# A top-256 search moved onto VectorE as a count over integers, with accumulator-freeing work given precedence

## The chip, the core and the metric

The kernel runs on one core of one Trainium2 chip. Five engines each work through their own queue of instructions in order: TensorE (PE in the rows; its weight loads are PEld), VectorE (DVE), ScalarE (ACT), GpSimd (POOL) and SyncE (SP), which mostly issues transfers. The metric is device microseconds of one execution, the median of several runs.

## What is computed

One layer of a hybrid encoder block over 1024 frames of width 1024, in float32. The part that matters here is the sparse attention: for each frame an index score over all earlier frames is worked out, the 256 best are kept, and attention looks at those alone.

```python
mod = silu(c) @ w_ada + b_ada                      # shift, scale, gate for both halves of the layer
h = rms_norm(x, g_mix) * (1 + sc1) + sh1
proj = h @ w_in                                    # attention columns, then RWKV columns
...
rel = relu(einsum('bthd,bsd->bths', q_idx, k_idx)) # 8 index heads
score_idx = einsum('bth,bths->bts', w_idx, rel)
score_idx = where(key_pos < limit, score_idx, -inf)
_, sel = top_k(score_idx, 256)                     # the search of this change
...                                                # softmax attention over the selected frames; RWKV-7 time mixing
x = x + gt1 * (concat(o_a, o_b) @ w_out)
u = relu(h2 @ w_ff1);  x = x + gt2 * ((u * u) @ w_ff2)
```

## The kernel before

The frames are worked on in two halves of 512 (hf 0 and 1). The program text goes: projection and RWKV of half 0; attention projections of half 0; index scores and search of half 0 (`indexer(0)`); RWKV projections of half 1 (`rwkv_proj(1)`); attention of half 0; RWKV of half 1; attention projections of half 1; then the output projection of half 0 and its feed-forward `ffn(0)`, with `indexer(1)`, attention of half 1, output projection and norm of half 1 hooked in at certain of its 64 units; and last `ffn(1)`.

The order of each engine's queue is fixed before the kernel runs. A planner walks the program with its own estimate of how long each instruction takes, and on each engine puts next whichever instruction is ready by that estimate and has the highest precedence. Precedence is the place in the program text: what stands earlier goes first, and later work fills the gaps. So the matrix products of `ffn(0)` fill TensorE while `indexer(1)` and attention of half 1, which stand earlier, run on other engines. At run time nothing is reordered: an instruction whose input is late holds up all behind it on its engine.

All big products go through `dense` (L389 to L399): for 128 output columns it takes eight weight tiles, split by ACT (L382) and POOL or DVE (L384) into a high and a low part, and runs 24 matmuls of 512 columns into one PSUM accumulator `ps_mm`, of which there are two. A product with its 24 matmuls is called a unit here. What empties the accumulator differs: in `shifted` (L419) ACT reads it (L422) and DVE reads it again (L426, L427); in `out_proj` DVE adds it to the residual (L1029); in the first eight units of each group of sixteen of `ffn`, ACT reads it with a relu (L1060), squares (L1074), rounds (L1075), and DVE subtracts (L1076); in the other eight DVE adds it to the residual (L1082).

The search (L846 to L913) finds for each frame, a row on one of 128 partitions, the 256th largest score. It does so bit by bit from 31 to 0: a candidate threshold is made, the scores at or above it are counted, and the bit is kept if at least 256 are. Half 0 has two blocks of rows (384 and 512 scores a row), half 1 four blocks (640, 768, 896 and 1024). In half 0 the first block and in half 1 the first two are counted by DVE; the others by ACT, with a sign and a running sum (L873). For the upper 16 bits DVE counts on a bf16 copy of the scores' upper halves (L858, L879, a one-source instruction), for the lower 16 on the scores themselves (L881, a two-source instruction with a tile of zeros). Small instructions of one or two columns (L870, L871, L888, L894 to L896) make the next candidates; DVE runs them for ACT's blocks too. After the search the masks are built (L914 to L928).

Of the kernel before, what the change touches and what calls it, by code (L numbers as in the profile page):

```python
# [15 lines left out]
HALF = 512  # L16
# [93 lines left out]
def body(tc, I, out, dbg=None):  # L110
# [305 lines left out]
        while held:  # L416
            nc.scalar.dma_start(*held.pop(0))

    def shifted(hf, hT, mi, col0, dst=None):  # L419
        ps = proj(hf, hT, OFF_B + col0, 128)  # L420
        t1 = dp.tile([128, HALF], F32, name="sh1", tag="sh1", bufs=2)
        A.activation(t1, ps, AF.Identity, scale=omu[:, mi:mi + 1])  # L422
        release()
        y = dst if dst is not None else dp.tile([128, HALF], F32, name="shy", tag="shy", bufs=2)
        mu = P("mu", mi, mi + 1)
        V.scalar_tensor_tensor(y[:, 1:HALF], ps[:, 0:HALF - 1], mu, t1[:, 1:HALF], ALU.mult, ALU.add)  # L426
        V.scalar_tensor_tensor(y[:, 0:1], lastp[:, hf, mi:mi + 1], mu, t1[:, 0:1], ALU.mult, ALU.add)  # L427
        if hf == 0:
            A.copy(lastp[:, 1, mi:mi + 1], ps[:, HALF - 1:HALF])
        return y  # L430
# [357 lines left out]
    def indexer(hf, ap, mp):  # L788
# [30 lines left out]
        for h in range(8):  # L819
# [5 lines left out]
            for b in blocks:  # L825
                W = width(b)
                s_ = sc[b]
                for c0 in range(0, W, 512):
                    n = min(512, W - c0)
                    ps = pst("f")  # L830
                    tq = slice(b * 128, b * 128 + 128)
                    mmul(ps[:, 0:n], qs[:, tq], kiH[:, c0:c0 + n], start=True, stop=False)
                    mmul(ps[:, 0:n], qs[:, tq], kiL[:, c0:c0 + n], start=False, stop=True)
                    rl = ap.tile([128, 512], F32, name="rl", tag="rl", bufs=3)
                    A.activation(rl[:, 0:n], ps[:, 0:n], AF.Relu)
                    if h == 0:
                        V.tensor_scalar(s_[:, c0:c0 + n], rl[:, 0:n], wn[hf][:, b, 0:1], None, ALU.mult)
                    else:
                        V.scalar_tensor_tensor(s_[:, c0:c0 + n], rl[:, 0:n], wn[hf][:, b, h:h + 1],
                                               s_[:, c0:c0 + n], ALU.mult, ALU.add)  # L840
# [2 lines left out]

        vb = [b for i, b in enumerate(blocks) if (i in VB if hf else i == VB0)]  # L846
        ab = [b for b in blocks if b not in vb]
        nv, na = len(vb), len(ab)
        jk = ap.tile([128, SW], BF16, name="jk", tag="jk", bufs=1)
        jka = ap.tile([128, SW], BF16, name="jka", tag="jka", bufs=1)  # L850

        def small(nm, n, dt=F32):
            return ap.tile([128, n], dt, name=nm, tag=nm, bufs=1)

        top = {}
        for b in vb:
            tp = ap.tile([128, width(b)], BF16, name=f"top{b}", tag=f"top{b}", bufs=1)
            V.tensor_copy(tp, sc[b].bitcast(BF16).rearrange("p (n two) -> p n two", two=2)[:, :, 1])  # L858
            top[b] = tp
        cv, cand, acc, pre, xm, xmh = (small("cv", nv), small("cand", nv, I32), small("acc", nv, I32),  # L860
                                       small("pre", nv, I32), small("xm", nv, I32), small("xmh", nv, I32))
        ca, canda, acca, prea, xma = (small("ca", na), small("canda", na, I32), small("acca", na, I32),
                                      small("prea", na, I32), small("xma", na, I32))
        zer = ap.tile([128, SW], BF16, name="zer", tag="zer", bufs=1)
        V.memset(zer, 0.0)
        V.memset(pre, 0)
        V.memset(prea, 0)
        for bit in range(31, -1, -1):
            if bit < 31:
                V.scalar_tensor_tensor(cand, pre, 1 << bit, xmh if bit >= 16 else xm, ALU.bitwise_or, ALU.bitwise_xor)  # L870
                V.scalar_tensor_tensor(canda, prea, 1 << bit, xma, ALU.bitwise_or, ALU.bitwise_xor)  # L871
            for i, b in enumerate(ab):
                A.activation(jka[:, 0:width(b)], sc[b], AF.Sign, scale=-1.0,  # L873
                             bias=0.0 if bit == 31 else canda.bitcast(F32)[:, i:i + 1], accum_out=ca[:, i:i + 1])
            for i, b in enumerate(vb):
                src = top[b] if bit >= 16 else sc[b]
                thr = 0.0 if bit == 31 else cand.bitcast(F32)[:, i:i + 1]
                if bit >= 16:
                    V.tensor_scalar(jk[:, 0:width(b)], src, thr, 0.0, ALU.is_ge, ALU.add, accum_out=cv[:, i:i + 1])  # L879
                else:  # L880
                    V.scalar_tensor_tensor(jk[:, 0:width(b)], src, thr, zer[:, 0:width(b)], ALU.is_ge, ALU.add,  # L881
                                           accum_out=cv[:, i:i + 1])

            for i, b in enumerate(ab):
                if bit == 31:
                    V.tensor_scalar(xma[:, i:i + 1], ca[:, i:i + 1], width(b) - 510.5, -1.0, ALU.is_gt, ALU.mult)
                else:
                    V.tensor_scalar(acca[:, i:i + 1], ca[:, i:i + 1], width(b) - 510.5, float(1 << bit),  # L888
                                    ALU.is_le, ALU.mult)
            if bit == 31:  # L890
                V.tensor_scalar(xm, cv, TOPK - 0.5, -1.0, ALU.is_lt, ALU.mult)
                V.tensor_scalar(xmh, xm, -65536, None, ALU.bitwise_and)
            else:
                V.tensor_scalar(acc, cv, TOPK - 0.5, float(1 << bit), ALU.is_ge, ALU.mult)  # L894
                V.tensor_tensor(pre, pre, acc, ALU.bitwise_or)  # L895
                V.tensor_tensor(prea, prea, acca, ALU.bitwise_or)  # L896
        V.tensor_tensor(cand, pre, xm, ALU.bitwise_xor)
        V.tensor_tensor(canda, prea, xma, ALU.bitwise_xor)
        for i, b in enumerate(ab):
            V.tensor_scalar(jk[:, 0:width(b)], sc[b], canda.bitcast(F32)[:, i:i + 1], 0.0, ALU.is_gt, ALU.add,  # L900
                            accum_out=ca[:, i:i + 1])

        up, lo16, cy = small("up", na), small("lo16", na, I32), small("cy", na)
        V.tensor_scalar(up, ca, TOPK - 0.5, None, ALU.is_ge)
        V.tensor_scalar(lo16, prea, 65535, None, ALU.bitwise_and)
        V.tensor_tensor(lo16, lo16, up, ALU.add)
        V.tensor_scalar(cy, lo16, 65535.5, None, ALU.is_ge)
        V.tensor_scalar(lo16, lo16, 65535, None, ALU.bitwise_and)
        V.tensor_scalar(prea, prea, 16, None, ALU.logical_shift_right)
        V.tensor_tensor(prea, prea, cy, ALU.add)  # L910
        V.tensor_scalar(prea, prea, 16, None, ALU.logical_shift_left)
        V.tensor_tensor(prea, prea, lo16, ALU.bitwise_or)
        V.tensor_tensor(canda, prea, xma, ALU.bitwise_xor)  # L913
        need = small("need", nb)  # L914
        for i, b in enumerate(blocks):
            W = width(b)
            th = (cand if b in vb else canda).bitcast(F32)
            ii = (vb if b in vb else ab).index(b)
            th = th[:, ii:ii + 1]
            gt = jk[:, 0:W]  # L920
            V.tensor_scalar(gt, sc[b], th, 0.0, ALU.is_gt, ALU.add, accum_out=need[:, i:i + 1])
            V.tensor_scalar(need[:, i:i + 1], need[:, i:i + 1], -1.0, float(TOPK), ALU.mult, ALU.add)
# [101 lines left out]
    def out_proj(hf, xT, mh, ml):  # L1024
        mark('oproj%d' % hf)
        GRP[0] = 4 + hf
        for d in range(8):
            ps = dense(I["w_out"], 0, 8, d * 128, 128, lambda k: mh[:, k, :], lambda k: ml[:, k, :])
            V.scalar_tensor_tensor(xT[:, d, :], ps, mod[:, 16 + d:17 + d], xT[:, d, :], ALU.mult, ALU.add)  # L1029

    def ffn(hf, xT, hT, fp, xp, hid, hooks={}):
        mark('ffn%d' % hf)
# [19 lines left out]
        for fg in range(FF // 128 // GF):  # L1052
            uh, ul = [], []
            for f in range(GF):
                hook(16 * fg + f)
                ps = dense(I["w_ff1"], 0, 8, (fg * GF + f) * 128, 128,
                           lambda k: hT[0][:, k, :], lambda k: hT[1][:, k, :])
                r = fp.tile([128, HALF], F32, name="ur", tag="s2", bufs=SB)
                if RL[hf] == "a":
                    A.activation(r, ps, AF.Relu)  # L1060
                else:
                    V.tensor_scalar(r, ps, 0.0, None, ALU.max)
                if f < 4:
                    ta, tb = (("shy", "fsq"), ("shy", "fsq"), ("sh1", "arn"), ("sh1", "cT"))[f]
                    a = dp.tile([128, HALF], F32R, name="uh", tag=ta, bufs=2)
                    b = dp.tile([128, HALF], F32R, name="ul", tag=tb, bufs=2 if f < 2 else 1)
                else:
                    a = hid.tile([128, HALF], F32R, name="uh", tag="uh", bufs=4)
                    b = hid.tile([128, HALF], F32R, name="ul", tag="ul", bufs=4)
                if SQ[hf] == "v":  # L1070
                    A.activation(a, r, AF.Square)
                    V.tensor_tensor(r, r, r, ALU.mult)
                else:
                    A.activation(r, r, AF.Square)  # L1074
                    A.copy(a, r)  # L1075
                V.tensor_tensor(b, r, a.bitcast(F32), ALU.subtract)  # L1076
                uh.append(a)
                ul.append(b)
            for d in range(8):
                hook(16 * fg + 8 + d)  # L1080
                ps = dense(I["w_ff2"], fg * GF * 128, GF, d * 128, 128, lambda k: uh[k], lambda k: ul[k])
                V.scalar_tensor_tensor(xT[:, d, :], ps, mod[:, 40 + d:41 + d], xT[:, d, :], ALU.mult, ALU.add)  # L1082
                if hf and fg == FF // 128 // GF - 1 and d in (5, 7):
                    store(d // 6)
        if not hf:
# [198 lines left out]
```

## Time and profile before

| What | Value |
|---|---|
| median of 3 runs | 1809.81 us (1807.12 to 1810.46) |
| the profiled execution, its own time | 1806.42 us |
| span of the profiled execution | 1804.6 us |
| TensorE busy, share of the span | 89% |
| VectorE | 64% |
| ScalarE | 48% |
| GpSimd | 27% |
| mean granted TensorE clock | 0.966 |

The span is the time from the first to the last instruction; the execution's own time is a little longer. Busy shares are averages over stages with different limits. Matmuls are pipelined, and one is shown as busy until its modelled end, so that a busy TensorE can still be slower than at its best: how many matmuls it ends in a stretch says more than its busy time.

### The profile page before, as it was taken

To read this page: it belongs to the slowest core of one execution; us is meant where nothing else is said; L and a number is where in the kernel's file an instruction comes from. 1 tells how busy PE (TensorE), PEld (TensorE's weight loads), DVE (VectorE), ACT (ScalarE), POOL (GpSimd) and SP (SyncE) were. 2 spreads that over 40 slices of the span, in tenths; PEclk is the share of its full clock that TensorE was granted. 3 is DMA by queue.
4 is the path that set the end of the run, shared out by engine and by line. 5 is a ranking of instruction groups with operands and counts; after the bars stand their busy time and mean duration, and the time that the engine had idled before them with its cause. 6 is when DMAs were issued, how large, how long until landed. Compare 5 with 4: busy or idle time off the path is not lost. (4 is left out here: it accounts for less than half of the span.)

```text
span 1804.6 us, 25007 instructions
## 1 busy us (share of the span) xinstructions
PE 1613.8 (89%) x8388; PEld 1206.4 (67%) x8388; DVE 1159.7 (64%) x2981; ACT 859.5 (48%) x1760; POOL 480.3 (27%) x391
## 2 busy tenths in 40 slices
PE   5996888898778988898987888999999999999998
PEld 3684655666554656665665676777886788888887
DVE  4788789956998779876899739773213333333333
ACT  3323353445556655344854783775335252525251
POOL 2445323334331143323223344111444300000000
PEclk9998899999989999999988998999999999999999
DMA  8896254225436533111212234223432343333332
GB/s 309 257 297 188 83 159 123 86 71 144 114 91 173 182 120 104 53 48 43 74 47 64 65 94 117 83 82 98 143 100 70 96 133 94 100 94 100 94 96 74
DMA packets 279493, 205.83 MB, mean 114 GB/s; under 512 B 33811, under 2 KB 234515, under 8 KB 279366
## 3 DMA queue, kind: packets, MB, share of 16 engines
q1 hardware_dynamic: 268610, 185.00, 34.5%
q10 hardware_dynamic: 10628, 19.24, 2.9%
q8 instruction: 66, 1.08, 0.3%
q14 instruction: 61, 0.50, 0.1%
q0 software_dynamic: 128, 0.01, 0.0%
HBM read 175.42 MB, written 28.78 MB: 113 GB/s over the span
## 5 line engine op out<-in xcount | busy, mean ns | idle before, releaser
L384 POOL TENSOR_TENSOR wlo<-wraw,whi 128x512 fp32r<-128x512 f32 x256 | 350.9, 1375 | 699.4 <-ACT whi L382 583.7
L119 PE MATMUL ps_mm<-hh,whi 128*128 128x512 f32 (+1 forms) x1024 | 421.9, 413 | 25.6 <-ACT whi L382 6.0
L119 PE MATMUL ps_mm<-hl,whi 128*128 128x512 f32 (+1 forms) x1024 | 420.4, 411 | 3.8 <-DVE hl L372 1.4
L119 PE MATMUL ps_mm<-hh,wlo 128*128 128x512 f32 (+1 forms) x1024 | 420.6, 411 | 3.5 <-POOL wlo L384 3.4
L382 ACT CAST whi<-wraw 128x512 fp32r<-128x512 f32 x384 | 235.1, 616 | 393.7 <-PE ps_mm L119 369.9
L119 PEld LDWEIGHTS ps_mm<-hh,whi 128*128 128x128 f32 (+1 forms) x1024 | 197.1, 193 | 74.5 <-ACT whi L382 13.5
L119 PEld LDWEIGHTS ps_mm<-hh,wlo 128*128 128x128 f32 (+1 forms) x1024 | 197.5, 193 | 47.6 <-POOL wlo L384 6.6
L119 PEld LDWEIGHTS ps_mm<-hl,whi 128*128 128x128 f32 (+1 forms) x1024 | 197.6, 193 | 47.3 <-issue 6.2
L119 PE MATMUL ps_mm<-uh,whi 128*128 128x512 f32 x512 | 205.0, 401 | 16.0 <-DVE pre L895 5.1
L119 PE MATMUL ps_mm<-ul,whi 128*128 128x512 f32 x512 | 204.8, 400 | 5.7 <-DVE ul L1076 5.7
L119 PE MATMUL ps_mm<-uh,wlo 128*128 128x512 f32 x512 | 203.8, 398 | 0.6 <-POOL wlo L384 0.6
L384 DVE TENSOR_TENSOR wlo<-wraw,whi 128x512 fp32r<-128x512 f32 x128 | 88.3, 690 | 130.1 <-ACT whi L382 130.1
L873 ACT ACTIVATE jka<-sc,canda 128x1024 bf16<-128x1024 f32 (+1 forms) x93 | 90.2, 970 | 89.8 <-DVE canda L871 77.4
L119 PEld LDWEIGHTS ps_mm<-uh,whi 128*128 128x128 f32 x512 | 97.8, 191 | 41.3 <-issue 9.7
L1082 DVE SCALAR_TENSOR_TENSOR xT<-ps_mm,mod,xT 128x512 f32<-128x512 f32 x64 | 47.9, 749 | 117.9 <-PE ps_mm L119 117.9
L119 PEld LDWEIGHTS ps_mm<-ul,whi 128*128 128x128 f32 x512 | 98.0, 191 | 29.2 <-DVE ul L1076 7.3
L119 PEld LDWEIGHTS ps_mm<-uh,wlo 128*128 128x128 f32 x512 | 97.8, 191 | 23.3 <-POOL wlo L384 1.1
L1076 DVE TENSOR_TENSOR ul<-ur,uh 128x512 fp32r<-128x512 f32 x64 | 44.0, 690 | 74.6 <-ACT uh L1075 74.4
L616 DVE TENSOR_TENSOR ytmp<-Lu,Y 128x60 f32<-128x60 f32 (+24 forms) x248 | 75.2, 303 | 6.1
L618 DVE TENSOR_TENSOR Y<-Y,ytmp 128x60 f32<-128x60 f32 (+24 forms) x248 | 73.6, 297 | 6.2
L981 DVE CUSTOM_DVE_ANT_0 L<-ps_f,mk 128x512 f32<-128x512 f32 (+3 forms) x96 | 51.9, 553 | 28.1 <-PE ps_c L999 17.0
L663 ACT COPY Ub<-ps_c 64x64 f32<-64x64 f32 x128 | 26.2, 205 | 83.7 <-DVE UV L661 76.3
(320 smaller groups left out, 2601.5 us busy)
## 6 DMA issues: line engine op xcount, KB each, us to landing
wraw<-in_w_ff_dram SPq DMA_DIRECT2D x256, 256.0 KB
wraw<-in_w_in_dram SPq DMA_DIRECT2D x92, 256.0 KB
mraw<-in_w_ada_dram SPq DMA_DIRECT2D x64, 256.0 KB
mraw<-in_w_ada_dram SPq DMA_DIRECT2D x16, 512.0 KB
wraw<-in_w_out_dram SPq DMA_DIRECT2D x32, 256.0 KB
rkvd<-shy ACTq DMA_DIRECT2D x24, 256.0 KB
xin<-in_x_dram SPq DMA_DIRECT2D x8, 512.0 KB
v<-rkvd SPq DMA_DIRECT2D x16, 256.0 KB
```

Of the source, the lines that this page charges most:

```text
L119: r = T.matmul(out, lhsT, rhs, start=start, stop=stop, **kw)
L382: (A.copy if HE[GRP[0]] == "a" else V.tensor_copy)(hi[:, :, 0:M], raw[:, :, 0:M])
L384: (V if LE[GRP[0]] == "v" or LE[GRP[0]] == "m" and GRP[1] else G).tensor_tensor(lo[:, :, 0:M], raw[:, :, 0:M], hi[:, :, 0:M].bitcast(F32), ...
L616: V.tensor_tensor(tv, Lu[:, c, 0:c].unsqueeze(2).to_broadcast([128, c, n]), Y[:, c, t0:8].unsqueeze(1).to_broadcast([128, c, n]), ALU.mult)
L618: V.tensor_tensor(Y[:, 0:c, t0:8], Y[:, 0:c, t0:8], tv, ALU.subtract)
L663: (V.tensor_copy if CE[2] == "v" else A.copy)(Ub[h * 64:h * 64 + 64, h, :], pu[0:64, h * 64:h * 64 + 64])
L873: A.activation(jka[:, 0:width(b)], sc[b], AF.Sign, scale=-1.0, bias=0.0 if bit == 31 else canda.bitcast(F32)[:, i:i + 1], accum_out=ca[:, ...
L981: V.tensor_tensor_reduce(L[:, c0:c0 + n], ps[:, 0:n], masks[b][:, c0:c0 + n], 1.0, -3e38, ALU.add, ALU.max, m2[:, pc:pc + 1])
L1076: V.tensor_tensor(b, r, a.bitcast(F32), ALU.subtract)
L1082: V.scalar_tensor_tensor(xT[:, d, :], ps, mod[:, 40 + d:41 + d], xT[:, d, :], ALU.mult, ALU.add)
```

## The change

The search is rewritten for all blocks on DVE, as a search over integers in two passes of 16 steps each. First two instructions a block turn each score's bit pattern, read as an integer, into one whose signed order is the order of the scores. The first pass finds the upper 16 bits: it counts on the upper halves, read in place as int16 with a stride of two (`halves(b)[0]`). Then two instructions a block make one float32 value out of what is left (the difference of the upper halves times 65536, plus the lower half), and the second pass searches that, in place, as float32. Each step is one one-source counting instruction per block and two small instructions over all blocks. ACT has no part in the search. The copies of the upper halves and the fix-up of ACT's blocks are gone. A multiplication in the score (L837) gets an added zero.

The other part: a helper `urgent()` raises the precedence of whatever stands inside it above all other work. It is put around what empties an accumulator: the rest of `shifted`, the additions of `out_proj` and `ffn`, and the relu, square, rounding and subtraction of `ffn`.

```diff
@@ shifted @@
+    def urgent():
+        return tc.high_priority(offset=1 << 20)
     def shifted(hf, hT, mi, col0, dst=None):
         ps = proj(hf, hT, OFF_B + col0, 128)
+        with urgent():
+            return shifted_out(hf, ps, mi, dst)
+    def shifted_out(hf, ps, mi, dst):
         t1 = dp.tile([128, HALF], F32, name="sh1", tag="sh1", bufs=2)
...
@@ indexer @@
-                        V.tensor_scalar(s_[:, c0:c0 + n], rl[:, 0:n], wn[hf][:, b, 0:1], None, ALU.mult)
+                        V.tensor_scalar(s_[:, c0:c0 + n], rl[:, 0:n], wn[hf][:, b, 0:1], 0.0, ALU.mult, ALU.add)
...
-        (L846 to L913, printed above, all but jk and zer)
+        dif = ap.tile([128, SW], F32, name="dif", tag="kir", bufs=1)
+        def halves(b):
+            x = sc[b].rearrange("p (n one) -> p n one", one=1)
+            return (x.bitcast(mybir.dt.int16)[:, :, 1], x.bitcast(mybir.dt.uint16)[:, :, 0])
+        for b in blocks:
+            W = width(b)
+            m, x = dif[:, 0:W].bitcast(I32), sc[b].bitcast(I32)
+            V.tensor_scalar(m, x, 31, 0x7fffffff, ALU.arith_shift_right, ALU.bitwise_and)
+            V.tensor_tensor(x, x, m, ALU.bitwise_xor)
+        cv, tv, nvv = small("cv", nb), small("tv", nb), small("nvv", nb)
+        def search(src, c0):
+            V.memset(cv, c0)
+            for it in range(16):
+                step = 2.0 ** (14 - it)
+                for i, b in enumerate(blocks):
+                    V.tensor_scalar(jk[:, 0:width(b)], src(b), cv[:, i:i + 1], 0.0, ALU.is_ge, ALU.add,
+                                    accum_out=nvv[:, i:i + 1])
+                V.tensor_scalar(tv, nvv, TOPK - 0.5, 2.0 * step, ALU.is_ge, ALU.mult)
+                V.scalar_tensor_tensor(cv, tv, step, cv, ALU.subtract, ALU.add)
+        search(lambda b: halves(b)[0], -0.5)
+        for i, b in enumerate(blocks):
+            d = dif[:, 0:width(b)]
+            V.tensor_scalar(d, halves(b)[0], cv[:, i:i + 1], 65536.0, ALU.subtract, ALU.mult)
+            V.tensor_tensor(sc[b], d, halves(b)[1], ALU.add)
+        search(lambda b: sc[b], 32767.5)
...
@@ out_proj @@
-            V.scalar_tensor_tensor(xT[:, d, :], ps, mod[:, 16 + d:17 + d], xT[:, d, :], ALU.mult, ALU.add)
+            with urgent():
+                V.scalar_tensor_tensor(xT[:, d, :], ps, mod[:, 16 + d:17 + d], xT[:, d, :], ALU.mult, ALU.add)
@@ ffn: `with urgent():` also around L1058 to L1076 @@
...
-                V.scalar_tensor_tensor(xT[:, d, :], ps, mod[:, 40 + d:41 + d], xT[:, d, :], ALU.mult, ALU.add)
+                with urgent():
+                    V.scalar_tensor_tensor(xT[:, d, :], ps, mod[:, 40 + d:41 + d], xT[:, d, :], ALU.mult, ALU.add)
```

## Rows read from the trace of the kernel before

**Rows 1.** First part of the page: busy time and share of each engine.
```profile
PE 1613.8 (89%) x8388; PEld 1206.4 (67%) x8388; DVE 1159.7 (64%) x2981; ACT 859.5 (48%) x1760; POOL 480.3 (27%) x391
```

**Rows 2.** Windows, all engines: us, busy PE, PEld, DVE, ACT, POOL; clock, DMA, GB/s.
```profile
453.00:550.00 97.00, 74.43 (x355) 52.56 (x354) 92.04 (x381) 52.80 (x118) 34.36 (x29) 0.91 0.36 102
...
914.00:1084.00 170.00, 138.76 (x545) 107.15 (x544) 127.60 (x387) 110.69 (x202) 63.25 (x45) 0.92 0.24 69
...
1402.00:1800.00 398.00, 397.14 (x1757) 324.52 (x1757) 143.54 (x210) 146.13 (x243) 14.45 (x11) 1.00 0.33 96
```

**Rows 3.** Windows of the accumulators ps_mm alone: PE (matmuls), PEld, DVE, ACT.
```profile
914.00:1084.00 170.00, 138.76 (x545) 107.15 (x544) 9.68 (x13) 5.24 (x9) 0.92 0.24 69
...
1116.00:1250.00 134.00, 47.21 (x147) 26.77 (x146) 0.00 (x0) 3.60 (x6) 0.97 0.29 84
1250.00:1402.00 152.00, 139.07 (x591) 109.15 (x589) 12.00 (x16) 4.75 (x8) 1.00 0.37 112
...
1530.00:1755.00 225.00, 225.00 (x987) 184.76 (x986) 12.77 (x17) 14.21 (x24) 1.00 0.33 96
```

**Rows 4.** Timeline of DVE in the search of half 1: start us, us, instruction.
```profile
943.32 0.74 DVE L1082 SCALAR_TENSOR_TENSOR xT<-ps_mm,mod,xT 128x512 f32<-128x512 f32 x1
...
944.05 1.01 DVE L879 TENSOR_SCALAR_CACHE_REDUCE jk<-top,cand 128x768 bf16<-128x768 bf16 x1
...
954.25 0.73 DVE L1082 SCALAR_TENSOR_TENSOR xT<-ps_mm,mod,xT 128x512 f32<-128x512 f32 x1
...
972.57 0.75 DVE L1082 SCALAR_TENSOR_TENSOR xT<-ps_mm,mod,xT 128x512 f32<-128x512 f32 x1
...
973.30 1.01 DVE L881 SCALAR_TENSOR_TENSOR jk<-sc,cand,zer 128x768 bf16<-128x768 f32 x1
...
979.26 0.75 DVE L1082 SCALAR_TENSOR_TENSOR xT<-ps_mm,mod,xT 128x512 f32<-128x512 f32 x1
```

**Rows 5.** Timeline of DVE where the search of half 1 ends.
```profile
1078.40 0.74 DVE L1082 SCALAR_TENSOR_TENSOR xT<-ps_mm,mod,xT 128x512 f32<-128x512 f32 x1
...
1084.06 0.87 DVE L921 TENSOR_SCALAR_CACHE_REDUCE jk<-sc,cand 128x640 bf16<-128x640 f32 x1
...
1089.48 0.74 DVE L1082 SCALAR_TENSOR_TENSOR xT<-ps_mm,mod,xT 128x512 f32<-128x512 f32 x1
```

**Rows 6.** DVE groups by shape, 914 to 1116 us: count, busy us, mean ns.
```profile
L879 DVE TENSOR_SCALAR_CACHE_REDUCE jk<-top,cand 128x768 bf16<-128x768 bf16 x15 | 15.2, 1012 | 0.3
...
L894 DVE TENSOR_SCALAR acc<-cv 128x2 int32<-128x2 f32 x31 | 11.0, 354 | 0.5
...
L1076 DVE TENSOR_TENSOR ul<-ur,uh 128x512 fp32r<-128x512 f32 x10 | 6.9, 689 | 0.4 <-ACT uh L1075 0.4
...
L921 DVE TENSOR_SCALAR_CACHE_REDUCE jk<-sc,canda 128x1024 bf16<-128x1024 f32 x1 | 1.3, 1267 | 0.0
...
L921 DVE TENSOR_SCALAR_CACHE_REDUCE jk<-sc,cand 128x640 bf16<-128x640 f32 x1 | 0.9, 874 | 0.0
```

**Rows 7.** Line L924 alone, whole span: duration ns least/median/greatest, and shapes.
```profile
L924 DVE TENSOR_SCALAR eq<-sc,cand x3: 414/608/1601, 517.7 to 1091.3; 128x384 bf16<-128x384 f32 x1, 128x640 bf16<-128x640 f32 x1, 128x768 bf16<-128x768 f32 x1
```

**Rows 8.** Timeline of DVE: a count and the small instructions behind it.
```profile
922.70 1.01 DVE L879 TENSOR_SCALAR_CACHE_REDUCE jk<-top,cand 128x768 bf16<-128x768 bf16 x1
...
923.75 0.17 DVE L894 TENSOR_SCALAR acc<-cv 128x2 int32<-128x2 f32 x1
923.95 0.16 DVE L895 TENSOR_TENSOR pre<-pre,acc 128x2 int32<-128x2 int32 x1
```

**Rows 9.** Timeline of POOL and DVE: a small instruction beside a weight split.
```profile
917.86 1.29 POOL L384 TENSOR_TENSOR wlo<-wraw,whi 128x512 fp32r<-128x512 f32 x1 [0.21 <-ACT whi L382]
917.91 1.25 DVE L870 SCALAR_TENSOR_TENSOR cand<-pre,xmh 128x2 int32<-128x2 int32 x1
```

**Rows 10.** DVE groups, 453 to 550 us: first and last of the search's nine largest.
```profile
L881 DVE SCALAR_TENSOR_TENSOR jk<-sc,cand,zer 128x384 bf16<-128x384 f32 x16 | 11.5, 720 | 0.4
...
L870 DVE SCALAR_TENSOR_TENSOR cand<-pre,xmh 128x1 int32<-128x1 int32 x15 | 3.5, 230 | 0.2
```

More of the change, by code (lines that the diff above doesn't have):

```diff
@@ L842, in indexer @@
             V.memset(sc[b][0:64, width(b) - 64:width(b)], -3.0e38)
-        vb = [b for i, b in enumerate(blocks) if (i in VB if hf else i == VB0)]
-        ab = [b for b in blocks if b not in vb]
-        nv, na = len(vb), len(ab)
         jk = ap.tile([128, SW], BF16, name="jk", tag="jk", bufs=1)
[L850 to L863, printed above, removed]
+        dif = ap.tile([128, SW], F32, name="dif", tag="kir", bufs=1)
         zer = ap.tile([128, SW], BF16, name="zer", tag="zer", bufs=1)
@@ L865, in indexer @@
         V.memset(zer, 0.0)
[L866 to L913, printed above, removed]
+        def small(nm, n):
+            return ap.tile([128, n], F32, name=nm, tag=nm, bufs=1)
@@ L916, in indexer @@
             W = width(b)
-            th = (cand if b in vb else canda).bitcast(F32)
-            ii = (vb if b in vb else ab).index(b)
-            th = th[:, ii:ii + 1]
+            th = cv[:, i:i + 1]
             gt = jk[:, 0:W]
@@ L1057, in ffn @@
                            lambda k: hT[0][:, k, :], lambda k: hT[1][:, k, :])
[L1058 to L1076, printed above, removed]
+                with urgent():
+                    r = fp.tile([128, HALF], F32, name="ur", tag="s2", bufs=SB)
+                    if RL[hf] == "a":
+                        A.activation(r, ps, AF.Relu)
+                    else:
+                        V.tensor_scalar(r, ps, 0.0, None, ALU.max)
+                    if f < 4:
+                        ta, tb = (("shy", "fsq"), ("shy", "fsq"), ("sh1", "arn"), ("sh1", "cT"))[f]
+                        a = dp.tile([128, HALF], F32R, name="uh", tag=ta, bufs=2)
+                        b = dp.tile([128, HALF], F32R, name="ul", tag=tb, bufs=2 if f < 2 else 1)
+                    else:
+                        a = hid.tile([128, HALF], F32R, name="uh", tag="uh", bufs=4)
+                        b = hid.tile([128, HALF], F32R, name="ul", tag="ul", bufs=4)
+                    if SQ[hf] == "v":
+                        A.activation(a, r, AF.Square)
+                        V.tensor_tensor(r, r, r, ALU.mult)
+                    else:
+                        A.activation(r, r, AF.Square)
+                        A.copy(a, r)
+                    V.tensor_tensor(b, r, a.bitcast(F32), ALU.subtract)
                 uh.append(a)
@@ L1081, in ffn @@
                 ps = dense(I["w_ff2"], fg * GF * 128, GF, d * 128, 128, lambda k: uh[k], lambda k: ul[k])
-                V.scalar_tensor_tensor(xT[:, d, :], ps, mod[:, 40 + d:41 + d], xT[:, d, :], ALU.mult, ALU.add)
+                with urgent():
+                    V.scalar_tensor_tensor(xT[:, d, :], ps, mod[:, 40 + d:41 + d], xT[:, d, :], ALU.mult, ALU.add)
                 if hf and fg == FF // 128 // GF - 1 and d in (5, 7):
```

## The prediction, made before the changed kernel was run

> **What bounds the kernel now.** I read the page's first part, then windows by stage, then the matmuls on the accumulators alone, then DVE's queue in the searches.
>
> TensorE is busy 89% of the span [rows 1]. From 1402 us to the end it never rests: 397 of 398 us [rows 2]. There 225 us hold 987 matmuls [rows 3]: 0.228 us each, so a unit of 24 takes 5.47 us. Attention of half 1 ends near 1250 us, and after it 591 dense matmuls, 24.6 units, still stand before 1402 us [rows 3]; `ffn(1)` follows. So behind the search of half 1 there is always dense work that could have run earlier, and each microsecond of it that TensorE misses during the search is paid at the end. That is the rule of the sum.
>
> The search of half 1 runs from 914 to 1084 us. At 5.47 us a unit, 170 us are 31.1 units; 545 matmuls are 22.7 [rows 3]. The missing 8.4 units are **45.8 us of TensorE lost**. The reader is to see why in DVE's queue. DVE is busy 127.6 of the 170 us [rows 2], nearly all of it up to 1022 us, and an accumulator is emptied when its instruction's place in that queue comes. Between the emptyings at 943.32 and 954.25 us stand seven counts of the one-source kind (four of 768, three of 640: 4992 scores) and 16 small instructions; between those at 972.57 and 979.26 us, four counts of the two-source kind (2816 scores) and 11 small ones [rows 4]. The queue is ordered ahead; one unit of dense work was reckoned to last as long as either list. But the first list takes 10.9 us and the second 6.7. TensorE needs 5.47.
>
> So the order reckons the one-source count too short. To put a number on it, take 5.47 less 0.72 for the emptying itself (the mean of 0.75 and 0.69 [rows 4, 6]): 4.75 us for a list. If the two-source count is reckoned at its true rate, 1.02 ns a score (below), the second list leaves 4.75 - 2.87 = 1.88 us for 15 instructions, about 0.12 each. Then the first leaves 4.75 - 23 x 0.12 = 1.99 us for 4992 scores: 0.40 ns each. The same sum where the masks begin: between 1078.40 and 1089.48 us [rows 5] stand 18 instructions, among them one-source counts on float32 of 896, 1024 and 640 scores, and three others of 640 that I put at 1.66 us; 4.75 - 2.16 - 1.66 = 0.93 us for 2560 scores, 0.36 ns each.
>
> **What a count takes on the chip.** L921 is the new counting instruction, on float32: 0.874 us for 640 scores and 1.267 for 1024 [rows 6], 1.02 ns a score. On 16 bits it is no faster: L879 takes 1.012 us for 768 bf16 [rows 6]. The plain comparison L924, the same instruction without the sum, takes 0.414 us for 384 and 0.608 for 768 [rows 7]: 0.505 ns. The sum costs the chip the double rate, and the order does not know it. The Trainium skill, "VectorE: DVE Perf Modes", section "The perf-mode tier table", gives `tensor_scalar` on SBUF four times the base rate in bf16 and twice in float32. L924 agrees for float32; the counting rows do not, so the measurement decides. By the page's rates this change would come out near rival D.
>
> **The search of half 1, after.** Four counts: the mean of the two ends, 1.07 us, times four, 4.28. Each starts its follower 0.04 us after its stated duration (922.70 + 1.01 against 923.75), and chained small ones follow at 0.2 us [rows 8]: 4.28 + 0.16 + 0.40 = 4.84 us a step. A small instruction can be held while POOL splits weights: 1.25 us beside a split of 1.29 [rows 9]; L894 has a mean of 0.354 against 0.17 undisturbed [rows 6, 8]. I add 0.25 for the two, 5.09 a step, 163 us for 32 steps. Conversions: on 3328 scores, two plain one-source instructions a block (0.505 ns a score and 0.22 fixed: 2.6 us each time) and two two-source ones (0.689 for 512 [rows 6], so about 1.04 ns and 0.15 fixed: 4.1), 13 us, and some 5 for collisions with POOL: 18. Together **181 us of DVE**, and 0.72 more for each unit emptied in between.
>
> **How many units come in between** is set by the order. It reckons a step at 3328 scores by its rate plus 6 x 0.12. At 0.5 ns, the chip's own rate without the sum and a little above the 0.36 to 0.40 read off, that is 2.38 us; at 1.02, 4.1. With 12 us reckoned for the conversions, 32 steps are 88 us, 18.6 units. In truth they take 181 + 13 = 194 us, in which TensorE does 18.6 x 5.47 = 102 us: **92 us lost, 47 more than before**. The bounds: at 0.36 ns, 15.3 units and 63 more; at 1.02 for all, 30.4 units and 9 fewer lost. The read of every second int16 has no row among the counts. It is nearest to L879, the same instruction on 16 bits, which is reckoned short; so I take it so. For the second pass rows 5 say the same of float32.
>
> Precedence for the emptying cannot mend this: it takes the first place that the order thinks right, and the places are too far apart in truth. It does keep the order from starving dense work, as DVE now has no gaps of its own.
>
> **The search of half 0.** DVE is busy 92.0 of 97 us there [rows 2]. The nine largest groups of the old search are 60.1 us [rows 10], with readouts 62.6. The new one has counts of 0.61 and 0.74, so 2.1 us a step, 66, and 5 for conversions. That is 8 us more DVE work, but ACT's tail is gone and the masks could be ready some 10 us earlier. I take nothing, between -10 and +8; attention of half 0 and the RWKV chain behind it hide or pass on the rest.
>
> **At nothing:** the added zero (ten passes of at most 512; even at the slow rate 0.26 us each). ACT's freed counting: ACT is busy 110.7 of the 170 us and would only help where DVE is done. Urgent work on ACT, and the stores that `shifted` releases there: they go earlier past other ACT work, at their old number. `out_proj` and `ffn` after 1402 us: DVE is busy 144 of 398 us [rows 2], so emptying waits for TensorE, not the reverse. If urgent additions delay the RWKV chain, eight of 0.75 us bound it at 6.
>
> **The sum:** the execution's own 1806.4 + 47 = 1853 us. The median of the runs stands 3.4 us above that execution, 0.2%, about what a measurement here can tell from no change; I leave it at 1853.
>
> **Rivals.**
> - B: the strided int16 pass is reckoned at its true rate, float32 is not. 16 steps at 4.1 and 16 at 2.38, with conversions 116 us, 24.4 units: 65 us lost, +19, 1825 us. For it: nothing shows how a stride is reckoned.
> - A, the other side: both passes are reckoned truly, 30.4 units, 37 us lost: 1797. It decides from 28.5 units on, where the loss falls under 46. Against it: rows 4 and 5; for it: ACT, which shared the blame for the old gaps, no longer waits in this chain.
> - D, also faster: the chip counts at the double rate. A step is 4 x 0.22 + 1.68 + 0.8 = 3.4 us, 139 us in all, 37 lost: 1798. Against it: the counting rows on both types.
> - E: precedence does not reach DVE's order. The search then has DVE to itself, TensorE stops after some three units: about 160 lost, over 1910.
>
> **Chances.** The forecast 0.42, B 0.27, A 0.13, D 0.04, E 0.03, something else 0.11. The range 1798 to 1870 takes in the forecast with its bounds (1843 to 1869), B, and the faster rivals' edge; outside it lie E, half of A and some of the rest. Faster: A, D and half of the rest, 0.22; within 0.2%: 0.06; slower: 0.72.
>
> **What would show it.** In the profile after: about 194 us from the first conversion to the masks of half 1; counts at 1.02 ns a score in both passes; two steps, some ten microseconds, between two emptyings; some 450 dense matmuls in that stretch, at under half of TensorE's best rate; ACT nearly idle there. B would show one step between emptyings in the first pass and two in the second. More than 28.5 units in the stretch, or a search under 150 us, would make me wrong.

## The result, and the profile after

The changed kernel takes 1828.72 us in the median of four runs (1827.13 to 1838.86), the kernel before 1809.69 beside it: a ratio of 1.0125, 95% interval 1.0094 to 1.0155. It is slower, by 19 us where 47 were forecast. The profiled execution has a span of 1825.6 us against 1804.6, 21.0 more. The first part of its page answers to [rows 1]:

```profile
span 1825.6 us, 24686 instructions
...
PE 1611.0 (88%) x8388; PEld 1207.1 (66%) x8388; DVE 1228.7 (67%) x2882; ACT 772.0 (42%) x1568; POOL 469.1 (26%) x391
```

ACT gave up 88 us, DVE took on 69, and PE does the same matmuls. Where the 21 us lie is read from windows cut at the same events in both kernels: the first instruction of half 1's search, its last small instruction, the last mask. First the dense matmuls alone (ps_mm on PE: us, busy us and count, clock, DMA share, GB/s), of the kernel before:

```profile
140.00:910.40 770.40, 378.14 (x1208) 0.96 0.36 107
910.40:1091.20 180.80, 147.68 (x581) 0.92 0.24 70
1091.20:1115.30 24.10, 21.63 (x87) 0.93 0.33 93
1115.30:1804.60 689.30, 579.07 (x2432) 0.99 0.33 98
```

and of the changed one:

```profile
140.00:928.50 788.50, 395.31 (x1278) 0.95 0.36 107
928.50:1124.70 196.20, 148.18 (x572) 0.88 0.22 63
1124.70:1155.00 30.30, 23.68 (x105) 0.93 0.28 78
1155.00:1825.60 670.60, 559.72 (x2353) 0.99 0.33 99
```

The first 140 us hold 384 dense matmuls in both, 4692 in all. The reader is to add up two things. The search starts 18.1 us later, but 70 more dense matmuls are done by then, 16 us of work at 0.228 each: nearly a wash. Search and masks together take 226.5 us for 204.9, 21.6 more, and only nine more matmuls are done in them (677 for 668): that is the loss. After the last mask it takes 18.7 us less, for 79 matmuls fewer (18 us). So the time is lost in the search of half 1 and its masks, as the prediction's sum has it. By that sum 196.2 - 572 x 0.228 = 65.8 us are lost in the search; the same windows give the kernel before 48.3. Of the 65.8, 48.0 us are time with no dense matmul at work, and 17.8 come from matmuls that took longer than 0.228 us (33.1 and 15.2 before), at a mean granted clock of 0.88 for 0.92. So most of the difference is work that was missing, as the prediction has it.

Why so few: DVE's groups by shape in that search (busy us, mean ns of one), which answer to [rows 6],

```profile
L880 DVE TENSOR_SCALAR_CACHE_REDUCE jk<-sc,cv 128x1024 bf16<-128x1024 int16 x16 | 20.4, 1278 | 0.5
L880 DVE TENSOR_SCALAR_CACHE_REDUCE jk<-sc,cv 128x1024 bf16<-128x1024 f32 x16 | 20.4, 1278 | 0.5
...
L880 DVE TENSOR_SCALAR_CACHE_REDUCE jk<-sc,cv 128x640 bf16<-128x640 f32 x16 | 14.1, 879 | 0.5
L880 DVE TENSOR_SCALAR_CACHE_REDUCE jk<-sc,cv 128x640 bf16<-128x640 int16 x16 | 14.1, 878 | 0.5
...
L882 DVE TENSOR_SCALAR tv<-nvv 128x4 f32<-128x4 f32 x32 | 9.2, 286 | 0.9
L883 DVE SCALAR_TENSOR_TENSOR cv<-tv,cv 128x4 f32<-128x4 f32 x32 | 5.2, 163 | 1.1
```

and from its timeline (start us, us, instruction) the first and last emptying that I counted in each pass, for [rows 4] (where ACT empties the accumulator, DVE's subtraction L1054 stands for the emptying):

```profile
949.37 0.75 DVE L1061 SCALAR_TENSOR_TENSOR xT<-ps_mm,mod,xT 128x512 f32<-128x512 f32 x1
...
1022.96 0.69 DVE L1054 TENSOR_TENSOR ul<-ur,uh 128x512 fp32r<-128x512 f32 x1
...
1044.79 0.69 DVE L1054 TENSOR_TENSOR ul<-ur,uh 128x512 fp32r<-128x512 f32 x1
...
1111.87 0.74 DVE L1061 SCALAR_TENSOR_TENSOR xT<-ps_mm,mod,xT 128x512 f32<-128x512 f32 x1
```

Each pair is eight gaps apart: 9.2 us in the int16 pass, 8.4 in the float32 pass, where TensorE needs 5.47 for a unit. In them stand 14 and 12 steps of the search, 1.75 and 1.5 a gap. The counts are alike in both passes to a nanosecond, 1278 and 879 ns for 1024 and 640 scores.

### The profile page after: what moved, and what is told of

It is laid out like the page before. It is cut to its first block, busy times and chain, and to the rows that moved or that the text cites. A ratio compares the mean times of both kernels' runs of the same rounds, so it can differ in the third digit from the quotient of the medians.

```text
span 1825.6 us, 24686 instructions
## 1 busy us (share of the span) xinstructions
PE 1611.0 (88%) x8388; PEld 1207.1 (66%) x8388; DVE 1228.7 (67%) x2882; ACT 772.0 (42%) x1568; POOL 469.1 (26%) x391
## 5 line engine op out<-in xcount | busy, mean ns | idle before, releaser
L384 POOL TENSOR_TENSOR wlo<-wraw,whi 128x512 fp32r<-128x512 f32 x256 | 340.5, 1335 | 765.4 <-ACT whi L382 644.5
L880 DVE TENSOR_SCALAR_CACHE_REDUCE jk<-sc,cv 128x640 bf16<-128x640 int16 (+3 forms) x192 | 181.2, 944 | 5.1
L1054 DVE TENSOR_TENSOR ul<-ur,uh 128x512 fp32r<-128x512 f32 x64 | 46.9, 733 | 73.6 <-ACT uh L1053 73.6
```

The source lines that it names most:

```text
L384: (V if LE[GRP[0]] == "v" or LE[GRP[0]] == "m" and GRP[1] else G).tensor_tensor(lo[:, :, 0:M], raw[:, :, 0:M], hi[:, :, 0:M].bitcast(F32), ...
L880: V.tensor_scalar(jk[:, 0:width(b)], src(b), cv[:, i:i + 1], 0.0, ALU.is_ge, ALU.add, accum_out=nvv[:, i:i + 1])
```

## The experiments

All times are medians; each ratio is to the kernel before on the same chip. "Lost" is the time of search and masks less 0.228 us for every dense matmul in them.

**1 and 2: the two parts apart.** `e1` is the old search with the precedence, `e2` the new search without it.

```diff
 e2:  def urgent():
-        return tc.high_priority(offset=1 << 20)
+        return contextlib.nullcontext()
 e1: the body of indexer() as in the kernel before, urgent() kept
```

> The kernel before with the precedence alone: the old search on bits, with VectorE and ScalarE sharing it, and the instructions that free a dense accumulator put first. Theory (the loss sits in the new search of half 1, where VectorE's order empties an accumulator only every 8.6 us): the precedence alone is worth little, 1805 to 1818 us. Rival (the precedence itself costs: in the changed kernel the mask chain of half 1 begins 20 us later): 1822 us or more.

> The changed kernel without the precedence: the new search on VectorE alone, and the dense emptyings at the planner's own priority. Theory: the planner still places about as many emptyings among the counts, since the counts wait for each other and the emptyings do not: 1822 to 1845 us, some 21 to 23 dense units in the search of half 1. Rival (only the precedence lets the emptyings in between the counts): over 1880 us, under 10 units in the search. Second rival (the precedence is what costs): 1815 us or less.

`e1`: 1803.92 us, ratio 0.9981 (0.9957 to 1.0005), a microsecond under its theory's range; its rival falls. `e2`: 1838.71, ratio 1.0176 (1.0121 to 1.023), as its theory had it. So the new search alone is worth about +30 us, and the precedence seems to take some 10 off it; the changed kernel was not measured beside `e2`, and the two intervals overlap. Both rivals of `e2` fall, the second by the time and the first by the count: without the precedence the search of half 1 holds 567 dense matmuls, with it 572. What the precedence does is seen ahead of the search: `e2` has 1180 dense matmuls between 140 us and its start, the changed kernel 1278; the start comes 10 us later for it.

**3 and 4: counts whose price the order was thought to know.** The forecast rests on the order reckoning the one-source count short and the two-source count truly. So the second pass (`e3`), then both (`e4`), were counted with two sources, in both halves; the edit of `e4`:

```diff
-                    V.tensor_scalar(jk[:, 0:width(b)], src(b), cv[:, i:i + 1], 0.0, ALU.is_ge, ALU.add,
-                                    accum_out=nvv[:, i:i + 1])
+                    V.scalar_tensor_tensor(jk[:, 0:width(b)], src(b), cv[:, i:i + 1], zer[:, 0:width(b)],
+                                           ALU.is_ge, ALU.add, accum_out=nvv[:, i:i + 1])
```

> The changed kernel with the second pass of the search (float32) counting by the two-source form with a zero operand, as the kernel before counted its low 16 bits; first pass, results and precedence as they are. The chip's price of a count should stay (1.04 ns a score for both forms). Theory (the order was planned with one-source counts at about 0.68 ns a score, and two-source ones at their true price, so more emptyings stand among them): 14 emptyings in the second pass for 10, 4 units of 5.47 us less lost, 1807 us (1802 to 1815). Rival (VectorE's load, now without ScalarE's share, is what costs): nothing changes, 1829 us.

> The changed kernel with both passes of the search counting by the two-source form with a zero operand. Theory: 33 emptyings in the search of half 1 for 22, so 11 units of 5.47 us less lost, and the search some 8 us longer by the emptyings' own time on VectorE: 1829 - 60 + 8 = 1777 us (1765 to 1795). If the two-source form over strided int16 is dearer on the chip than 1.04 ns a score, the gain shrinks by what the first pass gets longer. Rival (VectorE's load is what costs, or the loss sits outside the search): 1825 us or more.

My theory missed both times: 1847.16 us, 1.0234 (1.0173 to 1.0295), and 1894.64, 1.0455 (1.0406 to 1.0504). `e3`'s rival (nothing changes) missed too; `e4`'s time lies in its rival's range, and VectorE's own time is what got longer in it. The first half of the theory held: the order took in more units, and the search held 740 and 841 dense matmuls for 572 (ps_mm on PE, `e3`, then `e4`):

```profile
930.00:1152.70 222.70, 182.89 (x740) 0.92 0.25 73
945.60:1198.70 253.10, 206.31 (x841) 0.91 0.25 72
```

Two things undid it. First the chip's price. DVE's groups over the whole run, of `e3`

```profile
L881 DVE SCALAR_TENSOR_TENSOR jk<-sc,cv,zer 128x1024 bf16<-128x1024 f32 x16 | 28.4, 1773 | 0.3
...
L884 DVE TENSOR_SCALAR_CACHE_REDUCE jk<-sc,cv 128x1024 bf16<-128x1024 int16 x16 | 20.4, 1278 | 0.5
```

and the timeline of `e4`, with POOL beside DVE:

```profile
982.59 1.02 DVE L880 SCALAR_TENSOR_TENSOR jk<-sc,cv,zer 128x768 bf16<-128x768 int16 x1
982.75 2.01 POOL L384 TENSOR_TENSOR wlo<-wraw,whi 128x512 fp32r<-128x512 f32 x1 [2.61 <-ACT whi L382]
983.65 2.05 DVE L880 SCALAR_TENSOR_TENSOR jk<-sc,cv,zer 128x896 bf16<-128x896 int16 x1
985.53 1.30 POOL L384 TENSOR_TENSOR wlo<-wraw,whi 128x512 fp32r<-128x512 f32 x1 [0.78 <-ACT whi L382]
```

By these times the weight split on POOL waits for the count of 768 to end (2.01 us instead of 1.30), and the next count, 896 scores, then waits for the split: 2.05 us. The one-source count is not held: its mean is 1278 ns here as in the changed kernel. The Trainium skill, "SBUF — State Buffer", section "Who interferes with whom", says that a DVE instruction with two SBUF inputs contends with a GpSimd one that reads SBUF, and leaves `tensor_scalar` with an accumulator output out of the forms that can; both agree with these rows. The search grew from 196 to 223 and 253 us: its counts took 23 and 42 us more than one-source ones, and the emptyings let in some 5 and 8 (at 0.72 each). In `e4`, where half 0 searches so too, it also began 17 us later.

Second, dense work ran out. In `e4`, between the last mask and the last output of attention, these are all the dense matmuls there are:

```profile
1226.30:1355.40 129.10, 0.47 (x2) 0.88 0.23 61
```

The changed kernel has 137 there, the kernel before 144:

```profile
1155.00:1288.70 133.70, 45.15 (x137) 0.96 0.30 85
```

```profile
1115.30:1248.40 133.10, 46.31 (x144) 0.97 0.29 84
```

So the changed kernel has 2353 - 137 = 2216 behind attention, and the kernel before 2432 - 144 = 2288. `e3` and `e4` have 2253 - 141 and 2114 - 2, both exactly 2112. That number is a floor: 8 + 64 units of half 1's output projection and feed-forward are 1728, and 16 units more never moved forward. In the timelines of `e3` and `e7` sixteen emptyings of `ffn` stand right behind the eight of half 1's output projection, beside half 1's norm; by their place they are the last sixteen units of `ffn(0)`. So the changed kernel had only 104 matmuls left to put earlier, 24 us at 0.228, and the kernel before 176.

**5 and 6: the halves apart**, with the precedence: `indexer` takes the new body for one half, the old for the other.

```diff
+        if hf == 0:        # e6: hf == 1
+            (the new search)
+        else:
+            (the search of the kernel before)
```

> The changed kernel with the new search in half 0 alone; half 1 searches as before; precedence kept. Theory (half 0's search is short and has the chains of half 1 to hide behind, the cost is half 1's): within 5 us of the kernel before with precedence alone, 1800 to 1810 us. Rival (half 0 costs a share of the whole): 1812 us or more.

> The changed kernel with the new search in half 1 alone; half 0 searches as before; precedence kept. Theory: nearly all of the cost is here, 1822 to 1832 us. Rival (half 0 costs a share): 1817 us or less.

`e5`: 1801.03 us, 0.9959 (0.9937 to 0.9982). `e6`: 1828.90, 1.012 (1.007 to 1.0171), the changed kernel's time. Both are as the theory had them. The whole cost is half 1's search.

**7 and 8: the order held.** With the instructions as they are, each step of half 1's search is put behind one more emptying in DVE's queue, first in the changed kernel, then in the kernel before.

```diff
+    for n, x in enumerate(steps):                       # the first count of each step; e8: its candidate
+        tc.add_manual_dep(x.ins, empt[18 + n].ins.name,  # the emptyings in the program's order; e8: 14 + n
+                          mybir.DependencyInfo(mybir.DependencyClass.NoSync, mybir.DependencyReason.DATA), reason="order")
```

> The changed kernel, the order alone held: each of the 32 steps of half 1's search is made to stand behind one more emptying of a dense accumulator on VectorE's queue, 31 emptyings for 22; counts, their form and the results stay. First theory (what stands in the prediction: each dense unit let in is paid back 1:1 at the end): 9 units of 5.47 us less 9 x 0.72 us of VectorE's own time, 1829 - 49 + 7 = 1787 us. Second theory (after the first four runs: the dense work that does not need half 1's attention is 4692 - 2112 = 2580 matmuls in all, and only 104 were left behind the attention of the changed kernel; beyond them the chain from the start of the search to the end decides: 928 + 203 + 30 + 134 + 525 = 1820 us): 1813 to 1825 us, with none left behind the attention.

> The kernel before, the order alone held: each of the 31 later steps of half 1's search stands behind one more emptying of a dense accumulator on VectorE's queue, 31 for 24 as the chip ran them; no precedence, old search. Second theory (chain against stock of dense work): the search gets longer by some 7 x 0.72 = 5 us, the chain 910 + 186 + 24 + 133 + 525 = 1778 us is under the time, and the dense units let in are kept at the end until the stock is used up: 1785 to 1797 us. Rival (the emptyings are not what starves TensorE in the old search, ScalarE's counts are): 1805 us or more.

`e7`: 1827.29 us, 1.0098 (1.0065 to 1.013), 2 us above the second theory's range and 40 above the first theory's number. Its dense matmuls by the same windows:

```profile
927.20:1129.50 202.30, 192.10 (x816) 0.99 0.30 88
1129.50:1159.10 29.60, 20.58 (x77) 0.88 0.35 95
1159.10:1823.30 664.20, 498.79 (x2136) 0.96 0.31 91
```

and of the last window the part up to the end of attention, all engines but PE left out:

```profile
1159.10:1296.50 137.40, 7.38 (x24) 0.86 0.22 61
```

The queue's spacing was the cause of the gaps: with an emptying a step TensorE does 816 dense matmuls for 572 in a search only 6 us longer, at a clock of 0.99. And it is worth next to nothing. The 244 matmuls came out of the masks, the attention and what stood behind it: 24 are left in 137 us of attention, which is no shorter for it (133.7 us in the changed kernel), and 2136 - 24 = 2112 behind it. Even the 104 that left the stretch behind attention shortened it by 10 us (526.8 for 536.9), not by 24. They had covered the time in which the output projection's input is made ready, right behind attention; in `e7` ACT rounds the first of it at 1311.60 us (ps_mm on PE, first the changed kernel, then `e7`):

```profile
1288.70:1300.00 11.30, 9.54 (x39) 1.00 0.54 175
```

```profile
1296.50:1310.00 13.50, 0.00 (x0) 0.63 0.55 176
```

`e8` missed its theory: 1828.54 us, 1.0117 (1.0074 to 1.016), which lies in its rival's range. The search took in 798 dense matmuls for 581, but lasted 224.1 us for 180.8, not 186, and the floor of 2112 was met again. DVE was busy 170 us in it for 138, in longer two-source counts and longer small instructions, and waited longer for ACT's sums; first of `e8`, then of the kernel before:

```profile
L884 DVE SCALAR_TENSOR_TENSOR jk<-sc,cand,zer 128x768 bf16<-128x768 f32 x16 | 27.8, 1739 | 0.4
...
L899 DVE TENSOR_TENSOR prea<-prea,acca 128x2 int32<-128x2 int32 x31 | 14.3, 462 | 0.6
...
DVE acca L891 <- ACT jka L876: 44.2, 39, 1.5
```

```profile
L881 DVE SCALAR_TENSOR_TENSOR jk<-sc,cand,zer 128x768 bf16<-128x768 f32 x16 | 21.0, 1312 | 0.3
...
L896 DVE TENSOR_TENSOR prea<-prea,acca 128x2 int32<-128x2 int32 x31 | 7.9, 254 | 0.5
...
DVE acca L888 <- ACT jka L873: 36.3, 29, 3.0
```

In these groups the two-source counts took 8 us more than before, the small instructions of the search 20, the emptyings 6, and the waits for ACT 8 (the last lines: us in total, times, longest): about 40 of the 43 us. The search still lost 42.2 us, for 48.3, so `e8` does not tell its theory from its rival.

**9 and 10: a shorter old search.** In `e5`, DVE's two blocks of half 1 were through long before ACT's two, so one block was moved from ACT to DVE; `e10` also makes the low counts one-source.

```diff
-VB = (0, 1)
+VB = (0, 1, 2)
```

> The kernel with the new search in half 0 alone and the precedence, and in half 1's old search VectorE takes three of the four blocks (640, 768 and 896 scores) and ScalarE the one of 1024; each had two. In the run with the old split VectorE's two blocks were through at 1030 us and ScalarE's two only at 1086 us of a search that began at 920. Chain against stock: the search takes some 32 x 4.1 = 130 us for 178, the order holds 19 emptyings in it (104 us of TensorE), so 26 us are lost for 41; what the search no longer covers stays behind as dense work: 15 us less than 1801, 1780 to 1792 us. Rival (VectorE's three blocks starve the emptyings as the new search did): 1798 us or more.

> The same, and VectorE counts half 1's low 16 bits by the one-source form as well, which GpSimd's subtractions did not hold in any run so far (1.04 ns a score). The order holds 15 emptyings (82 us of TensorE) in a search of some 32 x 3.8 = 122 us: 40 us lost for 41 before, so about 1800 us by the count of units; by the length of the chain alone (56 us less) it would be under 1785 us.

Both slower than `e5`: 1818.77 us, 1.0073 (1.0033 to 1.0113), and 1818.82, 1.0063 (1.0038 to 1.0088). `e9` came out in its rival's range: the search took in 489 dense matmuls, 20.4 units for the 19 of the theory, but lasted 170 us, not 130: 8.3 us a unit, as in the new search (8.2). `e10` missed both of its numbers. In `e10`

```profile
921.50:1071.00 149.50, 107.25 (x378) 0.84 0.19 55
1071.00:1095.40 24.40, 20.27 (x87) 1.00 0.40 114
```

search and masks are 28 us shorter than in `e5`, with 465 dense matmuls for 682: 67.9 us lost for 46.1, 21.8 more, where the median rose by 17.8. Where the stock lasts, the length of the search does not count; what TensorE loses in it does.

**11 and 12: which part gains?**

> The kernel with the new search in half 0 alone and the precedence, measured again beside the one with the precedence alone. If the new search of half 0 is worth something of itself (its first run began half 1's search 8 us earlier than the run with the precedence alone): 3 to 8 us under the other, ratio to the kernel before under 0.998. If the gain is the precedence's alone: both alike, within 2 us.

> The kernel before with the precedence alone, measured again. By the first run a ratio of 0.9981 (0.9957 to 1.0005): between 1798 and 1806 us if the precedence is a small gain, 1806 to 1812 us if it is worth nothing.

1803.16 us, 0.9964 (0.994 to 0.9988), and 1803.12, 0.9971 (0.9951 to 0.9992). Alike: the gain of 0.3% is the precedence's, and half 0's new search is worth nothing that can be measured here. The precedence alone, on the old search, is the simplest version that comes out under both kernels, by a small margin: in `e1` the interval still reached 1.0005.

**All of them in one table** (of the profiled executions; us):

| kernel | search and masks | dense matmuls in them | lost | dense left behind attention, above 2112 | span | span - lost |
|---|---|---|---|---|---|---|
| before | 204.9 | 668 | 52.6 | 176 | 1804.6 | 1752 |
| after | 226.5 | 677 | 72.1 | 104 | 1825.6 | 1754 |
| e1 | 207.6 | 693 | 49.6 | 86 | 1801.7 | 1752 |
| e2 | 222.9 | 642 | 76.5 | 200 | 1833.6 | 1757 |
| e5 | 201.6 | 682 | 46.1 | 86 | 1792.9 | 1747 |
| e11 (as e5) | 203.2 | 683 | 47.5 | 86 | 1806.5 | 1759 |
| e12 (as e1) | 207.6 | 691 | 50.1 | 86 | 1801.3 | 1751 |
| e6 | 222.8 | 675 | 68.9 | 104 | 1819.0 | 1750 |
| e9 | 192.4 | 558 | 65.2 | 196 | 1820.5 | 1755 |
| e10 | 173.9 | 465 | 67.9 | 286 | 1809.7 | 1742 |
| e3 | 248.4 | 777 | 71.2 | 0 | 1842.4 | 1771 |
| e4 | 280.7 | 916 | 71.9 | 0 | 1880.8 | 1809 |
| e7 | 231.9 | 893 | 28.3 | 0 | 1823.3 | 1795 |
| e8 | 246.1 | 848 | 52.8 | 0 | 1826.3 | 1774 |

Where dense work is left, the span is 1742 to 1759 us plus what is lost, over losses from 46 to 77 us; one kernel's two executions, `e5` and `e11`, lie 14 us apart, so that spread may be mostly that of a single execution (median less loss gives 1751 to 1762). Where none is left the rule breaks, by some 20 to 57 us, and the chain decides: behind attention all four of these kernels take 525 to 528 us, the others 533 to 578. `e7` is 927 us to the start of the search, 232 for search and masks, 137 of attention and 527 behind it.

## Why the prediction was right, and where it was off

**The stage and the rule: right.** The cost is in half 1's search (`e6` carries it all), and it is TensorE's lost dense work, paid 1:1 at the end, as the table shows for the kernels that keep dense work in stock.

**The counts and the length: right.** 1.02 ns a score was forecast on both types; (1278 - 879) / 384 is 1.04, and the counts on int16 with a stride take what those on float32 take, to a nanosecond. Rival D falls. First conversion to end of search was put at 194 us and took 196.2. ACT is busy 47.8 us there, for 115.1 in the search before.

**"How many units come in between": the term that was mis-sized.** I reckoned 18.6 units and 92 us lost; the search held 572 / 24 = 23.8 and lost 65.8. These 26 us are the miss, 1853 against the profiled execution's 1827.4; what else was off cancels to a microsecond (the search before lost 48.3 us and not 45.8, the start and the masks, which I had left out, each cost 2 us more). The signs missed with it: 572 dense matmuls for the 450, a step and a half or somewhat more between emptyings for the two. The step that failed is the rate of 0.5 ns a score that I gave the order: 23.8 units are 130 us as the order reckons, less 12 for the conversions and 23.8 x 0.72 for the emptyings 101, so 3.16 a step, less 0.72 for the small ones 2.44 for 3328 scores, 0.73 ns. It is inferred from the spacing like the old one, on the premise that the order reckons a unit at 5.47 us; no run shows the order's own figures. The rows it came from had their own small instructions and ACT's chain in the same queue, and hung on the fixed 0.12 us for each instruction: with 0.05 the first list gives 0.72. The 0.12 came from taking the two-source count at its true rate, and `e4` does not bear that out: the same sum for its 35 units gives 1.23 ns, not 1.02. I had also set the value by what the chip does without the sum (0.505), which says nothing of the order. The range held the result in part by luck: 1829 lies under 1843, the lower end that I gave the forecast itself and for which no sum is shown, and it is inside the range only because that took in rival B.

**Rival B's number, not its mechanism.** B's 1825 us is what came, but B wanted one step between emptyings in the int16 pass and two in the other. The gaps are 9.2 and 8.4 us, with 1.75 and 1.5 steps.

**Precedence: taken at nothing beyond its place in the order; it is a small gain.** -5 and -7 us on the old search (`e1`, `e12`), some -10 on the new one (`e2` against the changed kernel, with intervals that overlap). It brings dense work ahead of the search (72 matmuls in `e1`, 98 on the new search), and the search starts later for it, 18 and 10 us. Rival E falls with the 572 matmuls of the changed kernel, and its premise with `e2`: the emptyings come in without precedence as well.

**Half 0 at nothing: right** (`e5` and `e6`, `e11` and `e12`).

**"Behind the search there is always dense work that could have run earlier": right for this change, wrong as a rule.** It held because the loss grew. For a gain it would have failed: there were 104 to 176 matmuls in stock, 24 to 40 us, and `e7` let in 10 units more without getting them back; the 104 that left the end brought 10 us there. Rival A's 1797 us for the changed kernel lies under what its chain allows: in `e7`, which comes nearest to A, the chain alone makes 1823.

## What to carry to other kernels

Filler that covers a long chain is a finite stock: before costing a chain by what its engine starves, count the filler left behind the chain, and see what it covers there; in these kernels only the starving cost while some was left, and the chain's length decided when none was. In a queue ordered ahead, a run of instructions that the order reckons too short starves whatever must come in between; the spacing of the emptyings in the trace shows it, but a rate taken from such gaps can be far off: here 0.36 to 0.40 ns was read off before and 0.73 after by the same sum, and the forecast should carry that. An instruction that lets more emptyings in can still be the worse choice if another engine holds it.

## What the runs showed of the hardware that was not expected

Beside GpSimd's weight splits a count of 1024 scores takes DVE 1.73 to 1.80 us in the mean with two sources (`e4`; 1.77 in `e3`) and 1.28 with one; the split in turn was stretched from 1.30 to 2.01 us. The one-source count with a sum has one price on float32, on bf16 and on int16 read with a stride of two, 1.04 ns a score and 0.21 us fixed, and in the changed kernel no single one of 1024 scores took over 1.282 us: it lacks the plain comparison's double rate [rows 7], but nothing held it in these runs. The plain comparison, without the sum, has no such steady price: in the kernel before one of 640 scores took 1.601 us, the greatest of [rows 7], where one of 768 took 0.608.
